# Attention maps turned by VectorE blocks and DRAM in place of TensorE transposes, with the rotation on GpSimd and a written-out TensorE order

## The chip, the core and the metric

The kernel runs on one core of a Trainium2 chip. Its engines are TensorE (PE in the profile; its weight loads are listed as PEld), VectorE (DVE), ScalarE (ACT), GpSimd (POOL) and SyncE (SP, which here only issues DMAs). Each engine takes its instructions in order; semaphores tie the engines together. The metric is the device time of one launch in microseconds; the figure of a kernel is the median of its runs.

## The reference

A trunk of two layers over 256 tokens of width 1024, all in float32. Each layer normalises x, multiplies it with one wide input projection, and runs two mixers side by side: a bidirectional chunked gated DeltaNet ("a") and differential attention ("b"). Both are gated, projected, merged and added to x. The change is in the attention and in what runs around it. Cut to that:

```
for l in range(DEPTH):                                  # 2 layers
    h = rmsnorm(x, norm_w[l]);  proj = h @ w_in[l]
    q_a,k_a,v_a,ab_a,z_a,q_b,k_b,v_b,z_b,gate_a,gate_b = split(proj)
    y_a = gated_delta_branch(q_a, k_a, v_a, ab_a, z_a, ...)
    # differential attention: 8 heads, two maps of 256 x 256 for each head
    q, k = partial_rope(q_b), partial_rope(k_b)         # 16 of 64 columns are rotated
    p = softmax(q k^T);  a = p[0] - lam * p[1];  o = a @ v_b
    y_b = rmsnorm(o) * (1 - lambda_init) * silu(z_b)
    merged = sigmoid(gate_a) * (y_a @ w_pa[l]) + sigmoid(gate_b) * (y_b @ w_pb[l])
    x = x + merged @ w_out[l]
return rmsnorm(x, final_norm_w)
```

## The kernel before

**Projections.** Activations and weights are split into a high and a low part (`hi`, `lo`), and each product is made of three TensorE matmuls, hi x hi, hi x lo and lo x hi. `weights` (L273) loads 256 rows of a weight at a time on SP into one of three raw buffers, casts them to `hi` on ScalarE (L308) and takes the rest into `lo` on VectorE (L310); of `hi` and `lo` there are two buffers each. `proj_tm` (L315) uses one such pair of 128-row steps: a *step* (kt) is three matmuls for each of two row tiles, six in all, and a projection of 512 columns has eight steps.

**Places.** In each layer, after q, k and v of both mixers, come ten projections of 512 columns: zb, za, gb, ga and pb, two each. Counted through, their steps are 0 to 79. All other TensorE work of the layer's middle part is fitted between them by step: `place(at)` (L1158) is the last matmul of step `at`, and an instruction made inside `behind(ins)` (L270) is issued on its engine not before `ins` has been. Within these bounds a planner, which simulates all engines, chooses the order on each engine; `tc.high_priority` moves an instruction ahead in its choice. `mark["pin"]` is the place for the parts of the DeltaNet.

**Attention.** `qk_part` (L594) evacuates q or k, rotates it with four VectorE operations (L602 to L605), and turns it with TensorE. For each head, `scores` (L1053) makes two score maps (L1061), their row maxima (L1069), exponentials with row sums (L1071), and the difference of the two maps (L1077). `turn` (L1081) turns that map with four TensorE transposes into a PSUM bank (L1088), which ScalarE copies into `aT` (L1090). `attend` (L1093) multiplies it with v (L1099): `aT` is the stationary operand (the weights), v the moving one. The scores of head h stand behind the transposes of head h - 1, the products of head h - 1 behind the scores of head h.

**DeltaNet parts in the same stretch.** `substitute` (L865) solves triangular blocks step by step on VectorE (L870, L871), spread over the weights of the qk, v, zb and za projections. `spread_blocks` sends the result to DRAM (`udr`, L878), and `merges` (L897) loads it back as `T64` (L905; for one half on POOL, for the other on SP) and into `U_` (L909, POOL). From step 41 on `merges` and `chunks` (L976) run on TensorE, beginning with y64p (L923).

**Bounces.** Some tiles are already turned by VectorE in 32 x 32 blocks and a trip through DRAM: `bounce` (L137) for v, `send` and `fetch` (L247, L254) for the gated attention output. Each is one write and four reads that POOL issues; the blocks' own turn is VectorE's (L135, L249).

Of the kernel before, what the change touches and what calls it, by code (L numbers as in the profile page):

```python
# [49 lines left out]
def hybrid_encoder(  # L50
# [53 lines left out]
    mark = {}  # L104
# [53 lines left out]
    def norm_row(w_row, nm):  # L158
# [14 lines left out]
        for i in range(3):  # L173
            mm = T.matmul(wb[i > 0], one if i else tri[:, 0, :], hl[:, i - 1] if i else row,
                          start=i < 2, stop=i != 1)
            tc.keep_in_program_order(mm)
# [138 lines left out]
    def proj_tm(act, w, c0, n, evac, nm, places=(None,) * 4, spare=(), later=None, turned=(), between=None,  # L315
# [3 lines left out]
        for kt, hi, lo in weights(w, c0, n, nm, places, later=later, spare=spare, turned=turned, held=held,  # L319
                                  first=first, raws=raws):  # L320
            for m in range(NM):
                ts_ = slice(m * P, (m + 1) * P)
                o = accs[m][:, :n]
                T.matmul(o, act[kt // 4][:, 0, kt % 4, ts_], hi, start=kt == 0, stop=False)  # L324
                T.matmul(o, act[kt // 4][:, 0, kt % 4, ts_], lo, start=False, stop=False)  # L325
                mark["proj"] = T.matmul(o, act[kt // 4][:, 1, kt % 4, ts_], hi, start=False,  # L326
                                        stop=kt == KT - 1).ins
                mark["done", nm, kt] = mark["proj"]
        if between:
            between()  # L330
        for m in range(NM):
            evac(m, accs[m][:, :n])
# [76 lines left out]
    for _ in range(5):  # L409
        mm = T.matmul(idle[:, :P], ones, ones, start=True, stop=True)  # L410
        tc.keep_in_program_order(mm)
# [22 lines left out]
    for m in range(NM):  # L434
        mm = T.matmul(pos_p[:, m : m + 1], pos_r[:, m * P : (m + 1) * P], ones[0:1, 0:1], start=True, stop=True)
        mark["pos"] = mm.ins
        tc.keep_in_program_order(mm)
# [69 lines left out]
    for l in range(DEPTH):  # L507
# [86 lines left out]
        def qk_part(s_, i):  # L594
                def evac_qk(m, ps):
# [6 lines left out]
                    V.tensor_tensor(r4[:, 0], x12, both(cos), ALU.mult)  # L602
                    V.tensor_tensor(r4[:, 1], x12, both(sin), ALU.mult)
                    V.tensor_tensor(x12[:, :, 0], r4[:, 0, :, 0], r4[:, 1, :, 1], ALU.subtract)
                    V.tensor_tensor(x12[:, :, 1], r4[:, 0, :, 1], r4[:, 1, :, 0], ALU.add)  # L605
                    pt = bank(f"qkt{l}{m}{s_}{i}")
                    for b in range(4):
# [4 lines left out]
                proj_tm(hT, wl, (C_QB, C_KB)[s_] + 512 * i, 512, evac_qk, f"qk{l}{s_}{i}",  # L612
                        turned=(0, 1) if (s_, i) == (0, 1) else ())
# [170 lines left out]
        def gram(nm, g, c, slot, after=None):  # L784
            gp = (bank if slot else bank_c)(f"{nm}{l}{g}{c}")
            for j4 in range(4):
                kqh = kq[:, 4 * g + j4, c]
                with behind(after):
                    mark[nm, g, c] = T.matmul(gp[:, j4 * P : (j4 + 1) * P], kqh[:, 0, :], kqh[:, slot, :],
                                              start=True, stop=True).ins  # L790
# [35 lines left out]
        def weigh_q(g, c, after):  # L826
            bv = B[:, c, 4 * g : 4 * g + 4]
            with tc.high_priority(offset=HP):
                gp = gram("kq", g, c, 1, after)
# [67 lines left out]
        def merges(g):  # L897
# [3 lines left out]
            G.memset(T64[blk(0), 0:8, 32:64], 0.0)  # L901
            G.memset(T64[blk(3), 8:16, 0:32], 0.0)
            for b in range(4):
                co = 32 * (b % 2)
                (nc.sync if g else G).dma_start(out=T64[blk(b), :, co : co + 32],  # L905
                                                in_=udr[1, b, g].rearrange("t j i -> j t i"))
            yield
            for b in range(4 if g == 0 else 0):
                G.dma_start(out=U_[blk(b), :, :, blk(b)].rearrange("j g t i -> j (g t) i"),  # L909
                                  in_=udr[0, b].rearrange("g t j i -> j (g t) i"))  # L910
# [5 lines left out]
            order = [(c, j4, mm, d) for c, j4 in every for mm in range(2) for d in range(2)]  # L916
            order.sort(key=lambda k: k != (0, 0, 1, 1))
            first = mark["pin"]
            for n_, (c, j4, mm, d) in enumerate(order):
# [464 lines left out]
```

## Time and profile before

| what | value |
|---|---|
| median of 3 runs | 749.98 us |
| lowest and highest run | 749.95 and 750.64 us |
| span of the profiled execution, first to last instruction | 748.5 us |
| TensorE busy | 739.3 us, 99% |
| VectorE busy | 586.5 us, 78% |
| ScalarE busy | 481.2 us, 64% |
| GpSimd busy (its DMA issues included) | 139.5 us, 19% |
| granted TensorE clock | 0.998 of full speed |

The busy shares are means over the whole span; what a microsecond of an engine is worth at one place is read from who waits there. A row of a timeline has the start, the duration, the engine, the line and operation, output<-inputs, the shape, and how many were merged; a bracket tells of idle time before it and what ended it. A matmul's record is longer than the spacing of matmuls, because they overlap. A product in float32 shows as two records. Groups of instructions end with busy time, mean nanoseconds of one, and idle time before them. Rows of DMA issues end with the size and the median time from issue to landing.

### The profile page before, as it was taken

How to read it: one execution, taken by the hardware profiler on the slowest of the kernel's cores; microseconds unless marked ns; L12 is line 12 of the kernel's file. 1: busy time of each engine (PE TensorE's matmuls, PEld its weight loads, DVE VectorE, ACT ScalarE, POOL GpSimd, SP SyncE). 2: the span in 40 equal slices, each digit the busy share in tenths (PEclk: the TensorE clock that was granted, in tenths of full speed). 3: DMA queues.
4: the chain of work that ended last, by engine and by line, in shares of the span. 5: the costliest groups of instructions: out<-in, count | busy, mean ns of one | idle time of the engine just before them, and what ended most of it. 6: DMA issues, size and time to landing. Idle time of an engine off the chain costs nothing.

```text
span 748.5 us, 13917 instructions
## 1 busy us (share of the span) xinstructions
PE 739.3 (99%) x5176; PEld 641.7 (86%) x5176; DVE 586.5 (78%) x1109; ACT 481.2 (64%) x1022; POOL 139.5 (19%) x221
## 2 busy tenths in 40 slices
PE   8999999999999999999999999999999999999996
PEld 6999889987888889888889899889778888998885
DVE  8696898999985965578668779999999679537782
ACT  6757875667876576645456578555687757566552
POOL 6004110112023440100000150202110425301000
PEclk9999999999999999999999999999999999999999
DMA  8754566776667462567674466767666748335641
GB/s 260 239 170 169 170 179 198 209 211 193 208 177 186 145 184 84 171 200 247 199 232 133 128 192 180 219 176 230 195 171 195 197 133 229 95 114 201 220 141 57
DMA packets 73734, 135.46 MB, mean 181 GB/s; under 512 B 12944, under 2 KB 13921, under 8 KB 73666
## 3 DMA queue, kind: packets, MB, share of 16 engines
q1 hardware_dynamic: 64750, 113.65, 50.6%
q0 software_dynamic: 7936, 19.35, 8.7%
q10 hardware_dynamic: 980, 1.58, 0.6%
q8 instruction: 41, 0.67, 0.4%
q14 instruction: 27, 0.22, 0.1%
HBM read 125.53 MB, written 9.01 MB: 180 GB/s over the span
## 4 chain that ended last, share of the span: by engine, by line
PE 95%; ACT 2%; issue 1%; DVE 1%; DMA 1%; SPq 0%; POOLq 0%; POOL 0%; DVEq 0%; ACTq 0%
PE pp_vb L369 4%; PE pp_qk L325 4%; PE pp_qk L326 3%; PE pp_qk L324 3%; PE sc L1061 2%; PE pp_o L369 2%; PE pf_k L385 2%; PE pp_za L325 2%; PE pf_v L385 2%; PE pf_v L389 2%; PE pp_gb L324 2%; PE pp_gb L325 2%; PE pp_zb L324 2%; PE pf_q L387 2%; PE pf_k L387 2%; PE pf_v L387 2%
## 5 line engine op out<-in xcount | busy, mean ns | idle before, releaser
L325 PE MATMUL pp_qk<-lo_qk,hT 128*128 128x512 f32 x128 | 50.5, 395 | 0.3
L326 PE MATMUL pp_qk<-hi_qk,hT 128*128 128x512 f32 x128 | 50.0, 390 | 0.0
L310 DVE TENSOR_TENSOR lo_qk<-raw_qk,hi_qk 128x1024 fp32r<-128x1024 f32 x32 | 39.1, 1222 | 11.6 <-ACT hi_qk L308 11.4
L324 PE MATMUL pp_qk<-hi_qk,hT 128*128 128x512 f32 x128 | 45.1, 393 | 0.0
L308 ACT CAST hi_qk<-raw_qk 128x1024 fp32r<-128x1024 f32 x28 | 29.4, 1049 | 23.4 <-PE pp_qk L326 12.4
L1071 ACT ACTIVATE es<-sc,mx 128x256 f32<-128x256 f32 x64 | 29.6, 474 | 19.5 <-DVE mx L1069 19.5
L387 PE MATMUL pf_q<-hT,hi_q 128*128 128x256 f32 x128 | 36.1, 286 | 0.0
L385 PE MATMUL pf_k<-hT,hi_k 128*128 128x256 f32 x128 | 36.1, 287 | 0.0
L385 PE MATMUL pf_v<-hT,hi_v 128*128 128x256 f32 x128 | 35.9, 285 | 0.0
L387 PE MATMUL pf_v<-hT,hi_v 128*128 128x256 f32 x128 | 35.8, 284 | 0.0
L385 PE MATMUL pf_q<-hT,hi_q 128*128 128x256 f32 x128 | 35.8, 284 | 0.0
L387 PE MATMUL pf_k<-hT,hi_k 128*128 128x256 f32 x128 | 35.8, 284 | 0.0
L310 DVE TENSOR_TENSOR lo_pb<-raw_pb,hi_pb 128x1024 fp32r<-128x1024 f32 x16 | 19.6, 1225 | 20.5 <-ACT hi_pb L308 20.2
L389 PE MATMUL pf_q<-hT,lo_q 128*128 128x256 f32 x128 | 35.2, 288 | 0.0
L389 PE MATMUL pf_v<-hT,lo_v 128*128 128x256 f32 x128 | 34.6, 288 | 0.0
L389 PE MATMUL pf_k<-hT,lo_k 128*128 128x256 f32 x128 | 34.3, 284 | 0.0
L308 ACT CAST hi_pa<-raw_pa 128x1024 fp32r<-128x1024 f32 x16 | 16.8, 1053 | 22.3 <-PE pp_pa L326 16.1
L679 DVE SCALAR_TENSOR_TENSOR cvq<-pf_q,cw,cvq 128x254 f32<-128x254 f32 (+1 forms) x64 | 30.0, 479 | 0.9 <-ACT cvq L675 0.3
L679 DVE SCALAR_TENSOR_TENSOR cvv<-pf_v,cw,cvv 128x254 f32<-128x254 f32 (+1 forms) x64 | 30.1, 482 | 0.1
L679 DVE SCALAR_TENSOR_TENSOR cvk<-pf_k,cw,cvk 128x254 f32<-128x254 f32 (+1 forms) x64 | 29.0, 478 | 1.3 <-ACT cvk L675 0.6
L325 PEld LDWEIGHTS pp_qk<-lo_qk,hT 128*128 128x128 f32 x128 | 24.0, 188 | 6.6 <-DVE lo_qk L310 1.6
L310 DVE TENSOR_TENSOR lo_pa<-raw_pa,hi_pa 128x1024 fp32r<-128x1024 f32 x16 | 19.6, 1224 | 11.1 <-ACT hi_pa L308 11.1
(414 smaller groups left out, 2542.2 us busy)
## 6 DMA issues: line engine op xcount, KB each, us to landing
raw_qk<-in_w_in_dram SPq DMA_DIRECT2D x32, 512.0 KB, 3.8
raw_k<-in_w_in_dram SPq DMA_DIRECT2D x16, 512.0 KB, 4.7
raw_q<-in_w_in_dram SPq DMA_DIRECT2D x16, 512.0 KB, 3.7
raw_v<-in_w_in_dram SPq DMA_DIRECT2D x16, 512.0 KB, 3.8
raw_zb<-in_w_in_dram SPq DMA_DIRECT2D x16, 512.0 KB, 3.7
raw_za<-in_w_in_dram SPq DMA_DIRECT2D x16, 512.0 KB, 3.7
raw_ga<-in_w_in_dram SPq DMA_DIRECT2D x16, 512.0 KB, 4.4
raw_pb<-in_w_pb_dram SPq DMA_DIRECT2D x16, 512.0 KB, 3.8
```

The source lines that it names most:

```text
L308: high = (V.tensor_copy if kp in turned else S.copy)(hi[:, :, :n], raw[:, :, :n]).ins
L310: mark[nm, kp] = high, V.tensor_tensor(lo[:, :, :n], raw[:, :, :n], hi[:, :, :n].bitcast(F32), ALU.subtract).ins
L324: T.matmul(o, act[kt // 4][:, 0, kt % 4, ts_], hi, start=kt == 0, stop=False)
L325: T.matmul(o, act[kt // 4][:, 0, kt % 4, ts_], lo, start=False, stop=False)
L326: mark["proj"] = T.matmul(o, act[kt // 4][:, 1, kt % 4, ts_], hi, start=False, stop=kt == KT - 1).ins
L369: mark["proj"] = T.matmul(o, act[kt // 4][:, pa, kt % 4, ts_], ws[kt][1 + pw], start=kt == 0 and n_ == 0, stop=kt == KT - 1 and n_ == 2).ins
L385: T.matmul(o, hi[:, cs], act[kt // 4][:, 0, kt % 4, :], start=first, stop=False, skip_group_check=True)
L387: T.matmul(o, hi[:, cs], act[kt // 4][:, 1, kt % 4, :], start=False, stop=False, skip_group_check=True)
L389: T.matmul(o, lo[:, cs], act[kt // 4][:, 0, kt % 4, :], start=False, stop=done, skip_group_check=True)
L679: V.scalar_tensor_tensor(ca[:, o0:o1], acc[:, b, o0 + sft : o1 + sft], cw[:, j, cb : cb + 1], ca[:, o0:o1], ALU.mult, ALU.add)
L1061: mm = T.matmul(sp[n][:, qt * SEQ : (qt + 1) * SEQ], qkT[h // 4][rows, 0, h % 4, qt * P : (qt + 1) * P], qkT[h // 4][rows, 1, h % 4, :], s ...
L1071: S.activation(es[:, n, qt, :], spv[:, qt, :], AF.Exp, bias=mx[:, n, qt : qt + 1], accum_out=s_all[:, h, n, qt : qt + 1])
```

## The change

What it does:

1. `turn` no longer uses TensorE or PSUM. VectorE transposes the 32 x 32 blocks of the finished map into the other half of the same tile, POOL writes that to DRAM (`att`), and four POOL reads bring it back turned, in runs of 64 floats, into `back` (tag w2a, two buffers). The two query tiles are interleaved, so that `attend` reads its weight operand with a step of two floats, 8 bytes.
2. The products with v are made eleven steps behind the scores (ten for the last head): scores at steps 4, 8, 13, ... 33, products at 15, 19, 24, ... 43. Before, transposes came about four steps and products about six behind.
3. The rotation of q and k is done by GpSimd.
4. From the first step of zb to the last of pb all matmuls (not the transposes of other parts) form one chain, each issued behind the one before it in the order of the program; the projections are generators that `drive` advances step by step, with the jobs planned for a step after it.
5. POOL's order is written out in part: the DMAs of `turn`, and the loads of `T64` and `U_` in `merges`, are issued behind one another (`mark["queued"]`).

The core of the diff; the renaming of loop variables and the same change of `T.matmul` inside `behind(mark["pin"])` into `mm` in the other parts of `merges` and `chunks` are left out:

```
+    mark = {"chain": None}
+    def mm(*args, **kw):
+        if mark["chain"] is None:
+            return T.matmul(*args, **kw)
+        with behind(mark["chain"]):
+            made = T.matmul(*args, **kw)
+        mark["chain"] = made.ins
+        return made
...
     def proj_tm(...):
-                T.matmul(o, act[kt // 4][:, 0, kt % 4, ts_], hi, start=kt == 0, stop=False)
+                mm(o, act[kt // 4][:, 0, kt % 4, ts_], hi, start=kt == 0, stop=False)
...
+            if kt == KT - 1:
+                for m in range(NM):
+                    evac(m, accs[m][:, :n])
+            yield
...
-                    V.tensor_tensor(r4[:, 0], x12, both(cos), ALU.mult)
-                    V.tensor_tensor(r4[:, 1], x12, both(sin), ALU.mult)
-                    V.tensor_tensor(x12[:, :, 0], r4[:, 0, :, 0], r4[:, 1, :, 1], ALU.subtract)
-                    V.tensor_tensor(x12[:, :, 1], r4[:, 0, :, 1], r4[:, 1, :, 0], ALU.add)
+                    G.tensor_tensor(r4[:, 0], x12, both(cos), ALU.mult)
+                    G.tensor_tensor(r4[:, 1], x12, both(sin), ALU.mult)
+                    G.tensor_tensor(x12[:, :, 0], r4[:, 0, :, 0], r4[:, 1, :, 1], ALU.subtract)
+                    G.tensor_tensor(x12[:, :, 1], r4[:, 0, :, 1], r4[:, 1, :, 0], ALU.add)
...
     def merges(g):
-            G.memset(T64[blk(0), 0:8, 32:64], 0.0)
-            G.memset(T64[blk(3), 8:16, 0:32], 0.0)
+            with behind(mark["queued"]):
+                G.memset(T64[blk(0), 0:8, 32:64], 0.0)
+                G.memset(T64[blk(3), 8:16, 0:32], 0.0)
             for b in range(4):
-                (nc.sync if g else G).dma_start(out=T64[blk(b), :, co : co + 32],
+                with nullcontext() if g else behind(mark["queued"]):
+                    (nc.sync if g else G).dma_start(out=T64[blk(b), :, co : co + 32],
...
             for b in range(4 if g == 0 else 0):
-                G.dma_start(out=U_[blk(b), :, :, blk(b)].rearrange("j g t i -> j (g t) i"),
+                with behind(mark["queued"]):
+                    mark["queued"] = G.dma_start(out=U_[blk(b), :, :, blk(b)].rearrange("j g t i -> j (g t) i"),
...
-        def turn(h, es, at):
-                ap_ = bank(f"at{l}{h}")
-                for qt in range(NM):
-                    for kt in range(NM):
-                            mark["at", h] = T.transpose(ap_[:, kt * SEQ + qt * P : kt * SEQ + (qt + 1) * P],
-                                                        es[:, 0, qt, kt * P : (kt + 1) * P], ident).ins
-                S.copy(aT.rearrange("p k q -> p (k q)"), ap_)
+        def turn(h, es):
+            V.transpose(es[:, 1].rearrange("p k (j t q) -> p (k j) q t", j=4, q=2),
+                        es[:, 0].rearrange("p q (x t) -> p x q t", t=32))
+            dd = dram.tile([NM, 4, 32, 4, 64], F32, tag="att", name=f"att{l}{h}", bufs=4)
+            with behind(mark.get("queued")):
+                G.dma_start(out=dd.rearrange("k i t j r -> (i t) k (j r)"), in_=es[:, 1])
+            back = work.tile([P, NM, 4, 64], F32, tag="w2a", name=f"aT{l}{h}", bufs=2)
+            for j in range(4):
+                with behind(mark.get("queued")):
+                    mark["queued"] = G.dma_start(out=back[blk(j)].rearrange("t k i r -> t (k i) r"),
+                                                 in_=dd[:, :, :, j].rearrange("k i t r -> t (k i) r")).ins
+            aT[h] = back
+        def attend(h):
+            op_ = bank(f"av{l}{h}")
+            av = aT[h].rearrange("p k i (t q) -> p q k (i t)", q=2)
+            for qt in range(NM):
+                for kt in range(NM):
+                    mm(op_[:, qt * P : (qt + 1) * P], av[:, qt, kt],
+                       vb[h // 4][:, kt, h % 4 * P : h % 4 * P + P],
+                       start=kt == 0, stop=kt == NM - 1)
...
+        for h in range(NH):
+            plan((4, 8, 13, 17, 21, 25, 29, 33)[h], attention, h)
+        for h in range(NH):
+            plan((15, 19, 24, 28, 32, 36, 40, 43)[h], attend, h)
+        mark["chain"] = mark["proj"]
+        for p in range(4):
+            drive([z_part((zb, za)[p // 2], (C_ZB, C_ZA)[p // 2], ("zb", "za")[p // 2], p % 2)], p)
...
+        for n, at in enumerate((39, 42, 44, 47)):
+            plan(at, weigh_q, n // 2, n % 2)
         order = [(mg, 41), (mg[:1], 43), (mg[1:], 45), (mg, 48), (mg, 50)]
         order += [(ch[i : i + 1], at + i) for at in (52, 54, 57, 59, 62, 64, 67) for i in range(2)]
         for gens, at in order:
             if at == 52:
-                key_sums()
+                plan(51, key_sums)
             for gen in gens:
-                run(gen, at)
+                plan(at, run, gen)
```

237 lines of the change are left out of this document (101 added, 136 removed).

## Prediction, made before the changed kernel was run

> **What bounds the kernel now.** I read the page's busy shares first, then the chain that ended last, then TensorE's order in time, and only then the engines that feed it.
>
> ```profile
> PE 739.3 (99%) x5176; PEld 641.7 (86%) x5176; DVE 586.5 (78%) x1109; ACT 481.2 (64%) x1022; POOL 139.5 (19%) x221
> ```
>
> TensorE (PE) is busy 99% of the span, so a microsecond taken off it shortens the kernel by one, and a wait put on it lengthens it by one. All else counts only through what it makes PE wait for. The chain shows the same around the change: it runs through PE's scores (sc) and products with v (av) one after another, and later through the first merge (y64p).
>
> ```profile
> 165.03 1.06 PE sc L1061 x8
> ...
> 172.66 1.06 PE sc L1061 x8
> ...
> 180.30 0.89 PE av L1099 x8
> ...
> 200.58 1.06 PE sc L1061 x8
> ...
> 240.17 1.39 PE y64p L923 x102
> ```
>
> A head's scores cost PE 1.06 us, its products 0.89 us (eight records of 0.11 us; an fp32 matmul has two). The engine to watch is VectorE (DVE). In the windows table, the columns after the bounds are length, then busy time of PE, PEld, DVE, ACT, POOL:
>
> ```profile
> 165.00:180.00 15.00, 15.00 (x79) 11.84 (x79) 15.00 (x31) 11.03 (x27) 2.73 (x5) 1.00 0.64 189
> ```
>
> While the first heads run, DVE has no free time either, and POOL (GpSimd) is nearly idle.
>
> **The transposes leave PE.** PE's order in time around one head's turn:
>
> ```profile
> 176.95 0.60 PE L1088 MATMUL at<-ident,es 128*128 128x128 f32 x4
> 177.30 0.48 PE L325 MATMUL pp_zb<-lo_zb,hT 128*128 128x512 f32 x1
> 177.62 0.39 PE L326 MATMUL pp_zb<-hi_zb,hT 128*128 128x512 f32 x1
> 177.85 0.40 PE L325 MATMUL pp_zb<-lo_zb,hT 128*128 128x512 f32 x1
> ```
>
> Starts count, since matmuls overlap. A projection matmul comes every 0.23 us (177.62 to 177.85). From the first transpose to the second matmul behind it is 0.67 us, of which one matmul is 0.23: four transposes cost 0.44 us. Sixteen heads (eight in each of two layers) give 16 x 0.44 = **7.0 us** off PE. ScalarE also loses sixteen copies out of PSUM; it is busy 64% and I count nothing for it.
>
> **What takes their place.** Each head now pays one block transpose on DVE, one write to DRAM and four reads back, the five DMAs issued by POOL, before av can start. The nearest rows are the bounces that the kernel already makes.
>
> ```profile
> L249 DVE STREAM_TRANSPOSE zb<-ob 128x512 f32<-128x512 f32 x8 | 8.4, 1092 | 0.1
> ...
> L135 DVE STREAM_TRANSPOSE tb_v<-thv 128x512 f32<-128x512 f32 x8 | 5.7, 712 | 0.0
> ...
> L602 DVE TENSOR_TENSOR r<-stg,sincos 128x128 f32<-128x128 f32 x16 | 4.6, 288 | 0.0
> L605 DVE TENSOR_TENSOR stg<-r 128x64 f32<-128x64 f32 x16 | 3.6, 225 | 0.0
> ```
>
> The transpose is of the same 128x512. L135 writes runs of neighbours (0.71 us), L249 writes every fourth element (1.09 us), the new one every second: I take 0.9, both ends for the range.
>
> ```profile
> bnc_v<-tb_v POOLq DMA_DIRECT2D x8, 256.0 KB, 3.4
> tb_v<-bnc_v POOLq DMA_DIRECT2D x32, 64.0 KB, 3.2
> ...
> T<-udr POOLq DMA_DIRECT2D x8, 64.0 KB, 4.5
> 170.90 2.17 POOL L142 DMA_DIRECT2D tb_v<-bnc_v  x4 [3.42 <-DMA bnc_v<-tb_v]
> ```
>
> The write is as large as bnc_v: 3.4 us to landing. Four reads take POOL 2.17 us to issue, so the last starts 1.6 us after the first. A read of 64 KB lands in 3.2 us when its runs are 512 bytes (tb_v) and in 4.5 us when they are 128 bytes (T); the new runs are 256 bytes, and I take 3.9. With 0.2 us for the hand-over and 0.5 us in DVE's and POOL's queues, from the finished map to the last landing it is 0.9 + 0.5 + 3.4 + 0.2 + 1.6 + 3.9 = **10.5 us**; with the low ends and no queue 9.1, with the high ends and one foreign set of four reads ahead on POOL 13.5.
>
> The Trainium skill, "DMA: Bandwidth & Descriptors", Specifications, asks for at least 512 bytes a transfer and says that shorter ones become read-modify-write; that speaks against the 256-byte runs. The two reads above agree in direction (4.5 against 3.2 us). By the rule the new read would be as slow as T, the trip 11.1 us, and with head 0's wait 0.6 us longer in each layer the sum 748.4; by tb_v's 3.2 us the trip is 9.8 us and the sum 745.8.
>
> **Does PE reach av before the data?** The map of a head is finished when the second L1077 of it ends.
>
> ```profile
> 174.56 0.89 DVE L1077 SCALAR_TENSOR_TENSOR es<-es,cc 128x256 f32<-128x256 f32 x2
> ...
> 183.01 0.90 DVE L1077 SCALAR_TENSOR_TENSOR es<-es,cc 128x256 f32<-128x256 f32 x2
> ...
> 205.12 0.88 DVE L1077 SCALAR_TENSOR_TENSOR es<-es,cc 128x256 f32<-128x256 f32 x2
> ```
>
> From the start of the scores that is 10.4 us for head 0 (165.03 to 175.45), 11.3 for head 1 (172.66 to 183.91) and 5.4 for head 4 (200.58 to 206.00). The plan sets av eleven steps behind the scores (ten for head 7). A step is six projection matmuls, 1.38 us; eleven are 15.2. To them come the head's own scores (1.06), two other heads' scores (2.12), for head 1 one av (0.89), for later heads two, and about 0.1 us at each change between kinds: 18.9 us for head 0, 19.7 for head 1, 20.6 later.
>
> Head 0 starts one step later than now, and its two last rotations, 2 x (288 + 225) ns each, leave DVE: I take 1.1 us off its 10.4 and 0.8 off head 1's 11.3. Head 0 then needs 9.3 + 10.5 = 19.8 against 18.9, a wait of 0.9; head 1 needs 21.0 against 19.7 + 0.9 already waited, 0.4. Head 4 needs 15.9 against 20.6: nothing. So 1.3 us a layer, **2.6 us** in both. Bounds: near nothing (trip 9.1) and some 5 a layer (trip 13.5, no help from the rotation: head 0 needs 23.9 against 18.9).
>
> **Strict order on PE.** From zb to pb every matmul is now issued behind the one before in the program. Today the planner puts both matmuls that need only `hi` ahead of the first that needs `lo`:
>
> ```profile
> 162.11 0.61 PE L324 MATMUL pp_zb<-hi_zb,hT 128*128 128x512 f32 x2
> 162.57 0.42 PE L325 MATMUL pp_zb<-lo_zb,hT 128*128 128x512 f32 x1
> 162.48 0.19 PEld L325 LDWEIGHTS pp_zb<-lo_zb,hT 128*128 128x128 f32 x1 [0.18 <-DVE lo_zb L310]
> ```
>
> PE could load `lo_zb` at 162.48, just in time for 162.57. In strict order it is wanted one matmul after 162.11, at 162.34, so that PE would stand for 0.1 us. I take four such a layer, **0.8 us** in all; nothing at best, and as the bad end every one of the sixteen weight pairs of z and gates by 0.2 us in both layers, 6.4.
>
> **POOL's and SP's queues.** The loads of T and U for the merges now stand behind the last read of head 6, and head 7's five DMAs behind U's.
>
> ```profile
> 222.79 3.15 POOL L909 DMA_DIRECT2D U__96<-udr  x4 [7.37 <-issue]
> ...
> 226.57 2.57 POOL L905 DMA_DIRECT2D T<-udr  x4
> ```
>
> The two take POOL 5.7 us, from 222.79 to 229.14, 11 us before y64p wants T at 240.17; that gap is the cover. Head 6's trip ends near there, so T slips by a few microseconds and stays covered; head 7's map, kept by up to those 5.7 us, loses the 3 to 5 us that the later heads have to spare. I take **0.8 us** in both layers (0 to 6).
>
> The next layer's small load (L622, `wab`) waits on SP for a buffer of tag w2a, which the returned maps now keep until av, and weight loads queue behind it. Three raw buffers, each good for two steps, cover it, so I count nothing; without that cover PE would wait once, by at most a step or two.
>
> **Rotation on GpSimd.** DVE loses about 1.03 us sixteen times.
>
> ```profile
> L116 POOL TENSOR_SCALAR_AFFINE_SELECT tri<-tri 128x128 f32<-128x128 f32 x2 | 0.5, 282 | 0.0
> ```
>
> The nearest POOL row of that size has one input and takes 0.28 us; four operations take 1.1 us by it and 2.2 if two inputs double it. POOL is 19% busy, and the q and k transposes behind it come several matmuls later in PE's queue, so I count nothing; if POOL stood in a DMA wait at each, about 1 us sixteen times.
>
> **The av weights with an 8-byte step.** The map is PE's weight operand, and now every second element is read.
>
> ```profile
> L1099 PEld LDWEIGHTS av<-vb,aT x128: 187/192/193, 179.9 to 605.5; 128*128 128x128 f32 x128
> ```
>
> No row shows a strided weight load. A load takes 0.19 us and overlaps the matmul before it; the pair comes every 0.11 us. I take no loss: the pair does not follow the load's duration today. If the step held back every load by 0.06 us, 128 of them would eat the 7.0 us; at 0.11 us, a pair at half the rate, they cost 14.1.
>
> The Trainium skill, "SBUF — State Buffer", in its note on cachelines, has lines of 16 bytes at full rate as long as two accesses fall into one; an 8-byte step leaves two fp32 values a line, so by it the load is free and rival D below has no chance. No run here shows it yet.
>
> **The sum.** 7.0 off; 2.6, 0.8 and 0.8 back: 2.8 us less. The span of the profiled execution:
>
> ```profile
> span 748.5 us, 13917 instructions
> ```
>
> The median of the runs is 749.98, 1.5 above it for what lies around the span. So 745.7 in a profile and **747.2 us** by the clock of the runs.
>
> **The rivals.**
>
> *A: PE hardly waits.* The trip is at its low end and POOL's queue is free: only the transposes go, 749.98 - 7.0 = 743.0. For it: heads 2 to 6 have some 4 us to spare, and two heads of eight decide. Against it: DVE's full window, in which these two lie.
>
> *B: DVE becomes the bound.* The transposes add 8 x 0.9 us a layer to a window without free time, of which the rotation gives back only its last pieces. Each stands once in front of a `lo` that today is ready just as PE wants it; at 0.4 us a head that is 3.2 a layer, 749.98 - 7.0 + 6.4 = 749.4: no change. Against it: the substitution (L870, L871) can give way, since DVE's load falls later.
>
> *C: slower, the trip through POOL's queue outlasts the distance.* Place: av of heads 0 and 1, and of head 7 behind T and U. Price: 5 us a layer at the long trip for the first two, 3 for head 7. It decides from 3.5 us of waits a layer, where the 7.0 are gone; halfway between there and 8, at 5.7, the time is 749.98 - 7.0 + 11.4 = 754.4. For it: POOL takes its instructions in order and sits idle in front of a read until the write has landed (the 3.42 us above), and v's last bounces still run when head 0 begins. Against it: heads 3 to 6 cannot come late by these rows.
>
> *D: slower, the strided weights.* 747.2 + 14.1 = 761.3 at half rate; it decides from 0.02 us a load, 2.8 us over 128.
>
> **How the numbers follow.** From no change this kernel's measurement can tell about 0.2%, 1.5 us (its runs spread over 0.7). Forecast 0.41, A 0.18, B 0.17, C 0.19, D 0.05. The forecast's own range is 744.5 to 749. Faster: nearly all of the forecast (0.38) and A, 0.56. Same: B and the forecast's upper end, 0.20. Slower: C and D, 0.24. For 8 in 10 the range runs from 742.3, just under A, to 754.5, the middle of C; what is left out is C's upper half and D.
>
> **What would show it.** The at group and the L1088 rows are gone, and the PE busy sum falls by 7 to 10 us. The wait table has PE at av behind a DMA, twice a layer, under 1 us each; av of heads 2 to 6 has none. PE's waits for `lo` in zb and za stay small. The weight loads of av take the same 0.19 us, eight products the same 0.89. POOL's rotation operations take 0.25 to 0.6 us. The prediction is wrong if PE waits at av for more than 3 us a layer (C), if lo waits add up to that (B), if av's products take over 1 us (D), or if the spacing of the heads has shrunk by the full 0.44 us with no wait anywhere (A).

## The result, and the profile after

| | before | after |
|---|---|---|
| median of the runs | 750.18 us (749.95 to 750.64) | 778.12 us (776.47 to 780.74) |
| ratio | | 1.037, 95% interval 1.036 to 1.039 |
| profiled execution: time, span | | 778.74, 777.0 us |
| TensorE idle inside the span, by the gaps between matmuls | 1.4 us | 25.2 us |

The kernel became 28 us slower; 747.2 was forecast, with 754.5 as the upper end. The median of the kernel before is of four runs here, that in the table ahead of the prediction of three of them. The page of the changed kernel, first the busy shares, then the chain that ended last by engine:

```profile
PE 744.3 (96%) x5112; PEld 639.5 (82%) x5112; DVE 591.3 (76%) x1061; ACT 475.2 (61%) x1006; POOL 227.8 (29%) x365
...
PE 75%; DVE 9%; POOL 5%; DMA 4%; issue 4%; ACT 3%; POOLq 0%; DVEq 0%; ACTq 0%
```

TensorE is no longer all of the chain. Its waits, by what ended them (total, times, longest):

```profile
PE av L110 <- DMA aT<-att: 15.2, 8, 4.2
PE y64p L110 <- DMA T<-udr: 4.6, 2, 2.5
PE pp_ga L110 <- DVE lo_ga L321: 2.2, 4, 0.8
PE qkt L618 <- POOL stg L615: 1.2, 2, 0.6
PE pp_zb L110 <- DVE lo_zb L321: 1.2, 3, 0.5
```

Together 24.4 us, of which 19.8 stand behind a DMA. TensorE's order in time shows the late operands of heads 2, 6 and 7 and of the first merge in layer 0 (heads 0 and 5 wait 0.8 us each; the y64p row ends with the view's window):

```profile
209.60 1.18 PE L110 MATMUL av<-vb,aT 128*128 128x128 f32 x8 [1.75 <-DMA aT<-att]
...
241.45 1.18 PE L110 MATMUL av<-vb,aT 128*128 128x128 f32 x8 [0.19 <-DMA aT<-att]
...
246.14 1.09 PE L110 MATMUL y64p<-T,A 32*32 32x32 f32 x78 [2.11 <-DMA T<-udr]
...
256.64 1.96 PE L110 MATMUL av<-vb,aT 128*128 128x128 f32 x8 [3.93 <-DMA aT<-att]
```

The last av takes 1.96 us instead of 1.18: TensorE's clock was halved there. The windows table, ahead of the wait at y64p, over the first merge, over the projection behind it, and from head 7's av on (third number from the right is the granted clock):

```profile
240.00:243.50 3.50, 3.31 (x19) 2.61 (x18) 2.28 (x2) 1.35 (x5) 3.41 (x7) 1.00 0.97 316
246.50:249.50 3.00, 3.00 (x112) 2.65 (x100) 0.00 (x0) 0.74 (x2) 0.19 (x1) 0.50 1.03 219
250.00:252.50 2.50, 2.50 (x16) 2.03 (x15) 1.13 (x1) 0.00 (x0) 0.00 (x0) 1.00 0.70 191
256.75:260.00 3.25, 3.25 (x99) 3.03 (x101) 0.10 (x1) 1.30 (x6) 0.00 (x0) 0.50 0.00 0
```

Layer 1 has one such stretch (635.6 to 639.0): three of 3.4 us at half clock, 1.7 us lost in each.

Why the operands are late is seen in GpSimd's order:

```profile
196.49 0.72 POOL L1086 DMA_DIRECT2D att<-es  x1 [2.25 <-ACT sqj L1105]
203.09 2.32 POOL L1090 DMA_DIRECT2D aT<-att  x4 [5.87 <-DMA att<-es]
...
219.30 1.56 POOL L886 DMA_DIRECT2D udr<-X  x2
220.85 0.76 POOL L1086 DMA_DIRECT2D att<-es  x1
221.59 1.14 POOL L886 DMA_DIRECT2D udr<-lt  x2
228.67 2.36 POOL L1090 DMA_DIRECT2D aT<-att  x4 [5.94 <-PE sc L110]
231.02 0.73 POOL L1086 DMA_DIRECT2D att<-es  x1
236.66 2.35 POOL L1090 DMA_DIRECT2D aT<-att  x4 [4.90 <-PE pp_gb L110]
...
239.64 2.57 POOL L915 DMA_DIRECT2D T<-udr  x4
...
242.87 3.12 POOL L920 DMA_DIRECT2D U__96<-udr  x4
245.98 0.72 POOL L1086 DMA_DIRECT2D att<-es  x1
252.60 2.34 POOL L1090 DMA_DIRECT2D aT<-att  x4 [5.91 <-issue]
```

For each head GpSimd stands up to 5.9 us in front of the reads until the write has landed. The next head's write is held behind these reads, T and U behind head 6's reads, and head 7's write behind U: it leaves at 245.98, though VectorE began to turn that map at 234.81. T leaves at 239.64, where the kernel before issued it at 226.57 (the projections are 3.5 us behind there).

Writes (att) and reads (aT) by the view of the DMAs, median time to landing last:

```profile
att<-es POOLq DMA_DIRECT2D x16, 256.0 KB, 5.0
aT<-att POOLq DMA_DIRECT2D x64, 64.0 KB, 2.8
```

The same for one head from the map on. Head 2's map is finished at 193.29 (192.42 + 0.88):

```profile
192.42 0.88 DVE L1074 SCALAR_TENSOR_TENSOR es<-es,cc 128x256 f32<-128x256 f32 x2
...
193.21 1.22 DVE L321 TENSOR_TENSOR lo_za<-raw_za,hi_za 128x1024 fp32r<-128x1024 f32 x1
...
194.64 0.68 DVE L410 SCALAR_TENSOR_TENSOR zb<-zb,pp_zb 128x512 f32<-128x512 f32 x1
195.24 0.71 DVE L1082 STREAM_TRANSPOSE es<-es 128x512 f32<-128x512 f32 x1
```

Three VectorE operations pass before the turn, it ends at 195.95; the write is issued at 196.49 and landed at 202.55, the reads follow from 203.09 to 205.41, the last landing is at 209.46. From the map that is 16.2 us.

**Where the 28.5 us of span went.** Sum the time from each matmul's start to the next one's start, by the block that it belongs to, in both traces (a wait counts to the block before it): gb 46.2 to 63.3 us, zb +5.9, ga +4.2, av +2.9, za +2.5, the last v projection before the late q and k transposes +1.6, turned maps 7.2 to 0, all else +1.6. By cause: -7.2 for the transposes, +24.4 waits, +5.1 half clock; 6.2 remain. Part of it is TensorE's refilling: at a wait of av, the time from the last projection matmul to av's second record is the wait and 0.24 us more than elsewhere; nineteen waits at that price would be some 4.5 us (an estimate). The strided products add 0.7 (below). The rest was not traced to a cause.

### The profile page after: what moved, and what is told of

The parts are those of the page before. It is cut to its first block, busy times and chain, and to the rows that moved or that the text cites. A ratio compares the mean times of both kernels' runs of the same rounds, so it can differ in the third digit from the quotient of the medians.

```text
span 777.0 us, 13992 instructions
## 1 busy us (share of the span) xinstructions
PE 744.3 (96%) x5112; PEld 639.5 (82%) x5112; DVE 591.3 (76%) x1061; ACT 475.2 (61%) x1006; POOL 227.8 (29%) x365
## 4 chain that ended last, share of the span: by engine, by line
PE 75%; DVE 9%; POOL 5%; DMA 4%; issue 4%; ACT 3%; POOLq 0%; DVEq 0%; ACTq 0%
PE pp_qk L108 8%; PE pp_pb L110 6%; PE pp_pa L108 6%; PE pp_za L110 5%; PE pp_ga L110 5%; PE pp_vb L380 4%; DMA aT<-att 3%; PE pp_o L108 3%; PE av L110 2%; PE pp_o L380 2%; PE pf_k L396 2%; PE pf_k L398 2%; PE pf_q L398 2%; PE pf_k L400 2%; PE pf_q L396 2%
## 5 line engine op out<-in xcount | busy, mean ns | idle before, releaser
L108 PE MATMUL pp_qk<-hi_qk,hT 128*128 128x512 f32 x256 | 81.1, 392 | 0.0
L1090 POOL DMA_DIRECT2D aT<-att x64 | 37.3, 589 | 74.1 <-issue 20.0
L108 PEld LDWEIGHTS pp_qk<-hi_qk,hT 128*128 128x128 f32 x256 | 47.4, 188 | 9.3
L110 PE MATMUL pp_ga<-hi_ga,hT 128*128 128x512 f32 x128 | 45.8, 408 | 0.0
L110 PE MATMUL pp_za<-hi_za,hT 128*128 128x512 f32 x128 | 43.8, 403 | 0.0
L110 PE MATMUL pp_pb<-hi_pb,ybT 128*128 128x512 f32 x128 | 42.7, 399 | 0.0
L110 PE MATMUL pp_zb<-hi_zb,hT 128*128 128x512 f32 x128 | 41.7, 396 | 0.0
L108 PE MATMUL pp_pa<-hi_pa,yaT 128*128 128x512 f32 x128 | 39.8, 389 | 0.0
L110 PE MATMUL pp_gb<-hi_gb,hT 128*128 128x512 f32 x112 | 39.2, 405 | 0.0
L110 PE MATMUL av<-vb,aT 128*128 128x128 f32 x128 | 19.7, 302 | 15.2 <-DMA aT<-att 15.2
```

The costliest lines, as they stand in the source:

```text
L108: return T.matmul(*args, **kw)
L110: made = T.matmul(*args, **kw)
L1090: mark["queued"] = G.dma_start(out=back[blk(j)].rearrange("t k i r -> t (k i) r"), in_=dd[:, :, :, j].rearrange("k i t r -> t (k i) r")).ins
```

## Experiments

The theories: **Q**, order in GpSimd's queue; **D**, transfers slowed by the load on the 16 DMA engines; **O**, the strict order on TensorE; with them the clock (C) and the rotation. These letters are not those of the prediction's rivals. All medians stand against 750.0 to 750.4 us of the kernel before on the same chip.

**e1_turn_on_pe and f1_turn_on_pe_early: without the trip.**

```
 def turn(h):                       # instead of V.transpose, write and four reads
+    for qt, kt: T.transpose(ap_[...], es[:, 0, qt, ...], ident)   # in the strict order
+    S.copy(back, ap_)
+plan((14, 18, 23, 27, 31, 35, 39, 42)[h], turn, h)      # e1: one step ahead of av
+plan((12, 16, 21, 25, 29, 33, 37, 40)[h], turn, h)      # f1: three
```

With the trip, the order `mark["queued"]` goes too: T's and U's loads on GpSimd stand behind nothing.

> The changed kernel with the maps turned on TensorE again (four transposes, one step ahead of each av, and ScalarE's copy); strict order, plan and the rotation on GpSimd stay. Theory Q (the loss is the trip of the maps through GpSimd's queue and what stands behind it): no wait at av and y64p is left, the halved clock goes, and what stays is 0.9 us twice at the q and k transposes behind the rotation and 1.6 us a layer for lo of ga: 750 + 1.8 + 3.2 = 755, between 751 and 757. Rival O (the strict order on TensorE is what costs): above 765. Rival B (VectorE short of time): GpSimd still has the rotation, VectorE loses the 11.3 us of block transposes; the ga waits for lo go too, 752.

780.93 us (779.72 to 781.47): missed, and by the time alone it would be rival O's. The waits show that this was the experiment's own fault:

```profile
PE av L110 <- ACT aT L1091: 16.1, 12, 2.1
```

ScalarE's copy was asked for too early, and in a strict order TensorE stands for it. With more room:

> The maps turned on TensorE again as in the first run, but three steps ahead of av instead of one, so that ScalarE's copy has 4.1 us (in the first run av waited for that copy twelve times, 16.1 us in all). Strict order, plan and the rotation on GpSimd stay. Theory Q/D (the loss lies in the trip through DRAM): what is left against the kernel before is 1.8 us at the q and k transposes, 1.3 for lo of zb and 2.4 for y1p behind ScalarE: 750 + 5.5, between 752 and 758. Rival O (strict order): 762 or more, with waits spread over many places.

760.45 us (758.47 to 763.29), in the middle between the two. No wait at av or y64p is left: 17.7 us less than the changed kernel although the transposes are back (6.1 by the sum of starts used above), so the trip costs some 24 us in all. But 10 us against the kernel before remain without any trip: 1.6 for the rotation (below) and some 8, by subtraction, that come with the strict order and its plan. Of the 7.9 us in its profiled execution the trace shows lo of zb 1.9 and y1p behind ScalarE 3.1:

```profile
PE y1p L110 <- ACT U__96 L976: 3.1, 2, 2.0
PE pp_zb L110 <- DVE lo_zb L321: 1.9, 4, 0.5
```

**e2_fill_waits: the clock.**

```
+for _ in range(4): mm(y64p bank's unused half, ident, tri)    # ahead of y64p, g == 0
+for _ in range(8): mm(av bank's unused half, ident, tri)      # ahead of av, h == 7
```

> The changed kernel with matmuls of no use put on TensorE into its two longest waits in each layer: four of 256 columns ahead of y64p and eight ahead of av of head 7 (about 0.44 us each, 1.8 and 3.5 us), into halves of PSUM banks that nobody reads. Theory C (a wait of some 2 us or more also halves the clock for about 3.4 us afterwards, 1.7 us of loss each, three times in the profile): the fillers lie in the waits of 2.1, 2.5, 3.9 and 4.2 us, the granted clock stays at 1.00 and the time falls by 3 to 5 us to about 773 to 775. Rival S (the clock falls because of the small 32x32 matmuls, or costs nothing): no change, 778, or up to 3 us more where a filler outlasts its wait.

777.33 us (775.88 to 779.72): the interval 1.034 to 1.039 covers that of the changed kernel, so the time decides nothing. The clock did what C says in the profiled execution (0.998; one of the others had 0.994):

```profile
243.50:247.00 3.50, 2.43 (x134) 2.16 (x134) 0.67 (x1) 0.75 (x2) 1.14 (x2) 1.00 1.05 262
247.00:252.00 5.00, 5.00 (x28) 4.40 (x27) 1.23 (x1) 0.00 (x0) 1.63 (x3) 1.00 0.62 180
253.00:258.00 5.00, 3.82 (x112) 3.21 (x111) 0.35 (x2) 2.25 (x9) 0.39 (x2) 1.00 0.10 24
```

The 32x32 matmuls run at 1.00 here, so they are not what halves it. One of the slow stretches lay ahead of a wait whose end GpSimd's queue sets, so by this reading it cost nothing; the other two are 3.4 us, about as much as the profiled span fell (777.0 to 773.8) and less than the runs scatter.

**e3_tu_on_sp and e4_write_on_sp: GpSimd's queue.**

```
-with behind(mark["queued"]): G.dma_start(T64 ...), G.dma_start(U_ ...)
+nc.sync.dma_start(T64 ...), nc.sync.dma_start(U_ ...)                 # e3
-with behind(mark.get("queued")): G.dma_start(out=dd..., in_=es[:, 1])
+nc.sync.dma_start(out=dd..., in_=es[:, 1])                            # e4
```

> The changed kernel with the eight loads of T and U for the first merge of each layer issued by SP instead of GpSimd, and no longer held behind the maps. Theory Q (order in GpSimd's queue): T no longer waits for head 6 and head 7's write no longer for U (7 us of GpSimd), so the waits at y64p (2.1 and 2.5 us) and at av of head 7 (3.9 and 4.2) go, and with them the halved clock (3 times 1.7): 778 - 4.6 - 8.1 - 5 = 760, between 757 and 765. Rival D (the 16 DMA engines are full there, busy share 1.0, whoever issues): the transfers land as late as now, 773 or more. Rival SP (weight loads held up behind the loads of T and U): new waits for hi or lo, over 770.

771.31 us (770.81 to 776.35). The waits at y64p and of head 7 are gone, as Q says, but the time is above Q's 757 to 765: 11.1 us of waits at av stay or are new,

```profile
PE av L110 <- DMA aT<-att: 11.1, 6, 2.8
```

now at heads 0, 2 and 6 in layer 0 and 0, 1 and 5 in layer 1, with four stretches at half clock behind them (clock 0.989). Rival SP's time is reached, but no weight is late.

> The changed kernel with only the write of each map (one DMA a head) issued by SP; the four reads stay on GpSimd, T and U too. Theory Q: a write no longer stands behind the reads of the head before and behind U, so it leaves when its map is turned; head 7's map is in DRAM long before U's loads are issued, its wait at av goes (3.9 and 4.2 us) with the halved clock, T comes a few us earlier: 760 to 766. Rival D (DMA engines full): under 4 us gained, 774 or more. Rival SP (weight loads wait behind a write that waits for its map): TensorE waits for hi or lo in z and gates, 778 or more.

767.90 us (766.09 to 769.49), just above Q's band: y64p and head 7 wait no more, no weight is late on SP, but heads 0, 2 and 5 wait in both layers,

```profile
PE av L110 <- DMA aT<-att: 12.5, 6, 3.0
```

since from the issue of their write to that of the first read it is still 5.3 to 9.4 us. Q is right for what it names, 7 and 10 us of the 28, and is not the whole.

**h2_half_weights: the load on the DMA engines.**

```
 raw = ...
-nc.sync.dma_start(out=raw[:, :, :n],  in_=w[rows, c0 : c0 + n])
+nc.sync.dma_start(out=raw[:, :, :n2], in_=w[rows, c0 : c0 + n2])   # n2 = n // 2, read twice by S and V
```

> The changed kernel with half of the bytes of the z and gb weights' loads left out (each row's first 256 columns are loaded and used twice; ScalarE, VectorE and TensorE do the same work as before). Queues, plan and trip stay. Theory D (the trip is long because its transfers share the 16 DMA engines with the weight loads): a map's write lands in 2.5 to 3.5 us instead of 2.6 to 7.3, a read in 2.1 to 2.5 instead of 2.1 to 5.8; heads 0 and 2 wait no more, the time falls by 6 us or more, to 765 to 772. Theory Q (order in GpSimd's queue alone: T and U behind head 6, head 7 behind U): y64p and head 7 wait as now, 775 to 779.

773.79 us (772.18 to 775.45): 4.3 less, between the two. The median write lands in 3.3 us instead of 5.0, a read in 2.3 instead of 2.8:

```profile
att<-es POOLq DMA_DIRECT2D x16, 256.0 KB, 3.3
aT<-att POOLq DMA_DIRECT2D x64, 64.0 KB, 2.3
```

Head 0 waits no more (0.8 and 2.4 us in the changed kernel), so it was late through D. For head 2 the run does not decide: 0.6 and 0.9 us in place of 1.7 and none. Head 5, y64p and head 7 still wait (1.2 to 4.0 us; their DMAs stand behind udr's writes, T and U), which D alone does not explain.

**f3_later_av and f4_later_and_sp: the distance.**

```
-plan((15, 19, 24, 28, 32, 36, 40, 43)[h], attend, h);  merges at 41, 43, 45, 48, 50
+plan((19, 23, 28, 32, 36, 40, 44, 47)[h], attend, h);  merges at 45, 46, 47, 49, 51
 # f4: and T, U and the maps' writes on SP, as above
```

> The changed kernel with only the plan moved: av of every head four steps (5.5 us) later (head 7 at step 47), the first merge's y64p at step 45 instead of 41 and what follows it by one to two steps. Queues as in the changed kernel. If the distance is what is short (the trips end 18 to 24 us after the scores for heads 0 to 6, 28 to 29 for head 7): heads 0 to 6 and y64p wait no more, head 7 by 1 to 3 us, the clock stays up: 752 to 758. Rival L (a wait moves on: ScalarE's and VectorE's work behind av comes later and gates ga and the merges): over 762.

760.87 us (760.02 to 763.54), 17 us less by moving steps alone, though above the 752 to 758 expected. Of all av only head 7's waits for its map, as expected, and a little more than the 1 to 3 us taken for it:

```profile
PE av L110 <- DMA aT<-att: 5.4, 2, 3.0
```

> Three edits together: av and merge later as in the run before, T and U loaded by SP, the maps' writes issued by SP. Theory Q with the longer distance: no wait at av, y64p or behind them; what stays is 1.8 us at the q and k transposes and 1 to 3 us for lo and y1p: 750 - 7.0 + 1.8 + 2 = 747, between 745 and 750. Rival SP (weight loads late behind waiting writes and T, U): 752 or more.

754.28 us (753.96 to 754.52), ratio 1.005 (1.004 to 1.007): no wait for the trip is left, and it is still 3.9 us slower than before, above Q's 745 to 750. The waits are

```profile
PE kq L110 <- DVE B L838: 2.5, 2, 1.6
PE pp_zb L110 <- DVE lo_zb L321: 1.3, 4, 0.5
PE qkt L618 <- POOL stg L615: 1.2, 2, 0.6
```

The 752 of rival SP is passed, and its mechanism shows in the first of these lines. The last weight of gb leaves SP at 236.01, behind T, U and a map's write (233.21 in f3, where GpSimd issues these), and lands at 241.62 (237.19 in f3). ScalarE waits for it, VectorE for ScalarE, and `B`, which kq waits for, stands behind that `lo` in VectorE's order:

```profile
241.72 1.05 ACT L319 CAST hi_gb<-raw_gb 128x1024 fp32r<-128x1024 f32 x1 [3.46 <-DMA raw_gb<-in_w_in_dram]
...
242.80 1.23 DVE L321 TENSOR_TENSOR lo_gb<-raw_gb,hi_gb 128x1024 fp32r<-128x1024 f32 x1 [5.74 <-ACT hi_gb L319]
243.94 1.22 DVE L838 TENSOR_TENSOR B<-kq,B 128x1024 f32<-128x1024 f32 x1
```

So the place of T, U and the writes on SP costs 2.5 us of waits there. Even without these the strict order with its plan, the rotation and the strided products would eat the 7.2 us that the transposes gave (7.2 + 3.9 - 2.5 = 8.6, by subtraction).

**g1_rotation_alone and g2_later_sp_rotation_back.**

```
-V.tensor_tensor(r4[:, 0], x12, both(cos), ALU.mult)      # and the three others
+G.tensor_tensor(r4[:, 0], x12, both(cos), ALU.mult)      # g1: in the kernel before; g2: back in f4
```

> The kernel before with one part of the change alone: the four rotation operations of q and k on GpSimd. In the changed kernel a set took 2.5 us there (0.50 + 0.55 + 0.78 + 0.69) and the last projection of each layer came 0.9 us later at the q and k transposes. If that is the rotation's own price: 750.2 + 1.8 = 752, between 751.2 and 752.8. As predicted before the change was seen (hidden): 750.2 within 0.5. If VectorE's 16.5 us less work helps TensorE elsewhere: under 749.5.

751.86 us (751.57 to 753.54), ratio 1.002 (1.001 to 1.003): the rotation costs 1.6 us by itself, as read from the trace. The prediction, which counted it as hidden, was wrong there.

> The combined kernel (later av and merge, T and U and the maps' writes on SP) with the rotation back on VectorE: 754.3 - 1.8 = 752.5, between 751.5 and 753.5. If VectorE is the bound in the window of the scores: the lo waits grow and the time stays at 754 or more.

760.42 us (755.41 to 762.29): worse, not better. With block transposes and rotation both on VectorE, lo of zb is late by 2.1 us in each layer:

```profile
PE pp_zb L110 <- DVE lo_zb L321: 4.2, 2, 2.1
```

Once the maps are turned on it, VectorE has no free time in that window (busy 17.00 of the 17.00 us from 165 to 182, in f4 too), and the rotation comes on top of this; the rotation's 1.6 us on GpSimd are the price of avoiding this. The waits are those of the profiled execution, which took 755.41 us; what made the median 5 us longer is not in the trace.

**Against the price of the strict order: g3_grouped_hi_first, g4_reads_on_sp, h1_hi_first.**

```
+for m: mm(hi x hi), mm(lo x hi)          # g3, g4: both row tiles; h1: in the strict order, all steps but a projection's last
+for m: mm(hi x lo)
+av at (21, 25, 29, 33, 36, 39, 44, 47)   # g3, g4, first merge at 44, rotation on VectorE as in g2
+att's reads on nc.sync                   # g4
```

> The kernel before this one, with two edits against the price of the strict order: in each step of a projection the four matmuls that need only hi stand ahead of the two that need lo (the waits for lo of zb were 0.65 us four times, 2.6 us), and av stands in the same step as a head's scores or a kq product, so that TensorE changes between projection and small products less often (0.09 us into a block, 0.09 to 0.11 out of it, about five changes a layer fewer, 2 us): 752.5 - 2.6 - 2 = 748, between 746 and 750.5. If the excess is not made of these two: 752 or more.

757.93 us (755.08 to 763.60): missed. In the profiled execution (763.60 us, 5.7 above the median) the wait for lo fell from 4.2 to 1.0 us, but v's projection now waits 3.2 us behind ScalarE's `stg`, kq 3.9 behind VectorE (the late weight on SP again: ScalarE waits 6.2 us for it) and scores 2.3 for `es`. Each cure of one wait moved another operand's date. And putting av next to other small products could gain nothing: in the kernel before, a block of av between projection matmuls takes 0.90 us by the starts, eight times the 0.112 of one product, so the change there is free; that of a block of scores costs about 0.2.

> As the kernel before this one, with the four reads of each map on SP as well, so that GpSimd carries nothing of the trip. If nothing on TensorE waits for the trip any more: the same time within 1 us, 747 to 749, whatever the trip then takes. Rival SP (reads wait for their write at the head of SP's queue, and weight loads behind them come late): TensorE waits for hi or lo, 752 or more.

767.45 us (764.42 to 768.44): the rival's time and its mechanism. kq waits 9.3 us behind VectorE (5.0 the longest), and half clock follows. VectorE is late because the last weight of gb leaves SP only at 240.59, behind T, U, and the maps' reads and writes (236.01 in f4): ScalarE waits 9.8 us for it, and VectorE's `lo` 10.0 us for ScalarE, with `B` behind it.

> The combined kernel (later av and merge, T and U and the maps' writes on SP, rotation on GpSimd; 754.3) with one edit: inside the strict order, each step of a projection but its last issues the four matmuls that need only hi ahead of the two that need lo. If the strict order's price lies in lo being wanted one matmul after hi (waits for lo of zb 0.5 us four times and of za 0.5 in its trace, with what they hold up 1.3 us a layer): 754.3 - 2 = 752, between 751 and 753.3. If it lies in the changes between projection and small products alone: 754 within 0.5.

755.92 us (754.88 to 756.67): no gain over f4, and above both expectations. The wait for lo of zb went from 1.3 to 1.1 us only, and two waits of scores for `es` of 1.1 us are new. The price of the strict order is not lo alone.

**f2_free_order, i1_free_paired, i2_free_paired_later_sp: without the strict order.**

```
-mark["chain"] = mark["proj"]
+mark["chain"] = None
+tc.keep_in_program_order(...)     # i1, i2: on seven of a head's eight scores
+                                  # i2: and f4's plan and queues
```

> The changed kernel with the strict order on TensorE taken away (the chain is never started); trip, queue and plan stay. Rival O (strict order turns every late operand into a wait of TensorE, a free order lets projection matmuls pass): below 765. Theory Q/D (the operands themselves come late, and the order that is planned ahead of time cannot know by how much): the waits at av and y64p stay within a few us of theirs, 772 to 785.

766.51 us (765.79 to 768.28): between. TensorE is idle 5.2 us in the whole span, and no wait at av or y64p is left: the planner let projections pass. It pays elsewhere. Scores come in blocks of four now:

```profile
160.17 1.13 PE L108 MATMUL sc<-qkT 64*128 64x256 f32 x4
161.23 0.73 PE L108 MATMUL pp_zb<-hi_zb,hT 128*128 128x512 f32 x2
161.90 1.13 PE L108 MATMUL sc<-qkT 64*128 64x256 f32 x4
```

Four of them, all of one row half, take as long as the eight did (1.13 us): the two row halves run side by side only when their matmuls alternate. Over the span the scores cost 12.6 us more.

> The changed kernel without the strict order, but with the eight matmuls of a head's scores kept together, as the kernel before has them. In the free order above each head's scores were cut in two blocks of four, each as long as the eight together (1.06 us): 1.06 x 16 = 17 us at most, 10.5 by the sum of the sc records. Theory O' (the strict order costs TensorE's waits, and only the cut scores hid that): 766.5 - 10.5 = 756, between 752 and 758. Rival (the work pushed behind pb is the loss): 762 or more.

767.70 us (767.38 to 768.37): missed, in the rival's range. Scores are still cut in part (+7.4 us against before), and the transposes of ya (+3.9) and pa (+2.5) now wait. 

> The kernel before this one with av and merge later and T, U and the maps' writes on SP. In a free order no wait was left in TensorE, so by theory O' these edits bring nothing more: 756 within 2. If the places of the work decide: any time between 748 and 766, in which case the order planned ahead is what differs and not the trip.

765.69 us (763.64 to 769.20): the places do decide, at the upper end of what was expected for that. In its profiled execution (769.20 us) TensorE waits 6.0 us at y64p for T, although its order is free. These three don't settle what the strict order costs, since without it the planner makes another kernel. f2 and i1 show that a free order can let other work pass a late operand at av and y64p; i2 shows that it does not always.

No version beat the kernel before. f4, the nearest of those with the trip, is 0.5% slower.

## Why the prediction was wrong

**Right.** The transposes' 7.0 us (the blocks fell from 7.2 to 0). A block transpose takes 0.71 us (0.9 taken). Strided weights cost little: 196 ns a load against 192. By the starts a product comes every 118 ns in place of 112 (112 also in f1, whose weights are not strided), 0.7 us over sixteen heads where the sum has nothing. By the view of the tile aT (nanoseconds least, median, longest; last line the reads' landing):

```profile
L110 PEld LDWEIGHTS av<-vb,aT x128: 193/196/333, 190.8 to 636.8; 128*128 128x128 f32 x128
...
DMA to landing us min/median/max: 2.1/2.8/5.8
```

(333 is under half clock.) The prediction's rival D, which needed 2.8 us to decide, is out, and the cacheline rule of the Trainium skill, "SBUF — State Buffer", by which this step is free, agrees but for these 6 ns. Its other rule that was weighed, short transfers in "DMA: Bandwidth & Descriptors", Specifications, does not show: in the changed kernel reads in 256-byte runs land in 2.1 us at best and 2.8 in the median, those of tb_v in 512-byte runs in 2.1 and 3.6. It is not ruled out either, since the two run under different load (in f3 3.9 against 3.5).

**The step that failed first: the trip, 10.5 us, and with it "heads 3 to 6 cannot come late".** The 2.6 us taken for heads 0 and 1 came out as 3.2, all of it head 0's; heads 2, 5 and 6, for which nothing was taken, wait 3.9. From the end of the second L1074 to the last landing of L1090 it took 13.2 us for head 0, 16.2 for head 2, 15.5 for head 5 and 22.8 for head 7 of layer 0. By its parts: the queues 0.5 us, in truth about 2 us of VectorE work ahead of the turn for heads 0 and 2 and 0.5 in front of the write; the write 3.4, in truth 5.0 in the median and up to 7.3; the hand-over 0.2, in truth 0.5. The read was put too high in the median (3.9 against 2.8), but head 2's last one took 4.6. The bound for the write was the median of another stage's bounces (bnc_v), and it did not rise with the load that the weights and the maps' own transfers put on the DMA engines here. And the sum took each head's trip by itself. In GpSimd's order it is not: a write stands behind the reads before it, and these behind their write.

**The step that failed by the most: T, U and head 7, 0.8 us taken, in truth 12.8.** y64p waits 2.1 and 2.5 us, head 7 3.9 and 4.2. The step said that head 6's trip ends "near there" and T slips "by a few microseconds". udr's writes (5.6 to 8.7 us to landing) stood in front of that trip, T left 13 us later, and head 7 paid the whole of it. Rival C names place and mechanism, but was priced at 5 and 3 us with bounds from undisturbed trips, and missed T itself, heads 2, 5 and 6. Its sign, more than 3 us a layer at av, came true: 7.4 and 7.8 us. e3 and e4, which each undo a part of this queue order, take 7 and 10 us off.

**Not in the sum at all: the clock.** Three stretches at half clock, 5.1 us of slower work, of which 3.4 reach the end by e2's reading; no time settled that. PE's busy sum, which was to fall by 7 to 10 us, rose by 5.0, from 739.3 to 744.3.

**Rotation: 0 taken, 1.6 measured.** The four operations take 2.5 us a set:

```profile
L614 POOL TENSOR_TENSOR stg<-r 128x64 f32<-128x64 f32 x16 | 12.5, 781 | 1.0
...
L615 POOL TENSOR_TENSOR stg<-r 128x64 f32<-128x64 f32 x16 | 11.1, 691 | 0.0
L613 POOL TENSOR_TENSOR r<-stg,sincos 128x128 f32<-128x128 f32 x16 | 8.8, 550 | 0.0
L612 POOL TENSOR_TENSOR r<-stg,sincos 128x128 f32<-128x128 f32 x16 | 8.0, 499 | 65.6 <-ACT stg L607 65.1
```

The cover ("several matmuls later") held fourteen times and failed once a layer, where 0.8 us is lost. The stated bound (1.1 to 2.2) was too low.

**Strict order: 0.8 taken, bounds to 6.4.** In the changed kernel the waits for lo are 3.4 us (zb 1.2, ga 2.2). The early turn on TensorE puts the order near 8 us with its plan, beyond the upper end: lo of zb and y1p behind ScalarE are 5.0 of it, the rest is not traced. The step counted lo alone.

**B.** As a bound VectorE did not show in the changed kernel (lo waits 3.4 us in both layers, where B needed 6.4); g2 shows that it would have in the window of the scores, had the rotation stayed on it.

## To carry to other kernels

An operation that is taken off the bounding engine and replaced by a trip through DRAM is priced by its latency under the load of that stage, and by everything that is issued behind it on the same queue: write, landing and read of one trip, times the trips in a row, against their spacing. Where the bounding engine runs in a strict order, every operand has a date, and a mean margin does not help; put the distance at the longest trip that the stage's own DMAs show, not at the median. Moving such DMAs to another queue moves the price with them: on SP they made a weight late. And a wait of 2 us or more on TensorE (in h1 one of 1.1) is to be priced with the half clock that may follow.

## What the hardware showed

TensorE's granted clock changes on a grid of its own. In the changed kernel the slow stretches begin at 246.5, 256.7 and 635.6 us and each ends 3.4 us later; 246.5 to 256.7 is three times 3.4. A gap of 2.11 us that lay within one such window (244.0 to 246.1) halved the clock of the next one, while gaps of 2.44 and 2.46 us in layer 1 (from 570.1 and 623.6), which by that grid are split over two windows, did not. The Trainium skill, "TensorE: Matmul & The Clock Gate", Part 1, tells of a free-running window of 3.4 us and half rate after an idle one; the trace agrees with the window and the rate, but a window that was idle for 2.1 of its 3.4 us was enough. In all the traces, counting idle time between matmul records, every window inside a kernel that was idle for 56% or more was followed by half rate (21 windows), of those idle for 53 or 54% two of three, and of those below that, when they ran at full rate themselves, a single one. That one, in h1 ahead of 561.5 us, has only a gap of 1.1 us among scores of 64 rows, so idle time between matmuls is not the whole rule.

Scores of 64 rows run two at a time when the row halves alternate (eight in 1.06 us) and alone otherwise (four in 1.06).
